# The shared expert of a mixture of experts moved behind the routed experts, in a one-core kernel of two transformer blocks

## The chip, the core and the metric

The kernel runs on one core of a Trainium2 chip. A core has a matmul engine (TensorE; PE in the profile, with its weight loads as PEld), a vector engine (VectorE, DVE), an activation engine (ScalarE, ACT), a general engine (GpSimd, POOL), a queue engine that issues most of the transfers (SyncE, SP), and sixteen DMA engines that all issuing engines share. The metric is the device time of the whole program in microseconds (us), lower is better. All times of the trace count from the start of the span.

## The reference, cut to what matters

Two blocks follow each other on 512 rows of 1024 columns. The first ends in a mixture of experts; the second is a different transformer block (two layers) that starts from the first one's output. The part that the change touches, cut:

```python
x = layernorm(DN_ALPHA * x + g1 * mix, ln1_w, ln1_b)
h = layernorm(x) * (1 + sc2) + sh2
scores = sigmoid(h @ router_w)          # 512 x 64, 8 experts of 64 are chosen for each row
...
def body(acc, blk):                     # blocks of 128 rows of one expert
    tok, wt, e = blk
    xb = h[tok]
    hid = silu(xb @ w1[e]) * (xb @ w3[e])
    return acc.at[tok].add(wt[:, None] * (hid @ w2[e]))
routed = scan(body, zeros(h.shape), blocks)
shared = (silu(h @ sw1) * (h @ sw3)) @ sw2
x = layernorm(DN_ALPHA * x + g2 * (routed + shared), ln2_w, ln2_b)
```

The shared expert has the size of one routed expert (1024 to 256 and back), but works on all 512 rows, four tiles of 128.

## The kernel before

Each 128 x 128 by 512 product is made of three passes over fp32 data that was split in a high and a low part (`mm3`, lines 128 to 130). A weight granule is 1 MB (128 x 2048 fp32): SyncE loads it (L1181), ScalarE casts its high part (L122), VectorE subtracts to get the low part (L123). An expert has three granules: two for gate and up (`hidden`, 24 matmuls of 128 x 512, the `gu` tiles), one for down (`down`, 12 matmuls, the `y` tiles). Raw granules live in a small ring, and a load waits until the split has freed its slot.

`mix_out` is the stage between the token mixer and the experts. Its steps stand in the tuple `MIX`: load and split the output projection's weights (`l`, `w`, four granules `wo0` to `wo3`), transpose its inputs (`y`), load x and row vectors (`m`), project (`o`), normalise a tile (`n`: x, then h, which goes to `hrows` in DRAM), transpose h (`t`), route it (`r`: the `rt` matmuls, the selection of 8 experts on VectorE, the prefix matmuls `pl`, `place`), begin the first expert (`b`: the selection of its 128 rows, `sel`, and the gather), and load (`e`) and split (`E`) the first experts' granules early. The shared expert has steps of its own here: `L` and `W` load and split its granules `shg0` to `shg2`, and `("s", t)` does row tile t from the transposed h that the router also uses, and writes the result `yosh` to `yrows[0]`, and x to `yrows[1]`. A scheduler then sets the order on each engine, so the tuple is not the order of execution.

Then come 65 jobs in 39 groups: four static experts (e0 to e3), ranked ones, and pairs that share one gather. A group gathers 128 rows of h from `hrows` by a GpSimd DMA (L1690, tile `xg`), transposes them (`tsp`, 8 matmuls) and splits them (`xh`, `xl`); each job multiplies; VectorE scales the result by `g2b` (`yo`, L1444); a GpSimd DMA adds the rows into `yrows[b % 2]` (L1694). Behind e1's first matmuls the experts are put in order of their counts (`cnts`, `ot`, `ord`), and SyncE reads from it which weights to load for the ranked experts (`ids`).

After the last pair (e63, e64, with the down granule `eg2`) a loop for overflowing experts is passed (L1636), which runs no iteration here. Then `combine` loads `yrows[1]` into x (L1610) and `yrows[0]` into y (L1613), adds them (L1618), and normalises (`l2st`, `l2rs`); the second block's first steps (`nm0d`, `nm0p`, `pi`) follow.

Of the kernel before, what the change touches and what calls it, by code (L numbers as in the profile page):

```python
# [13 lines left out]
F32 = mybir.dt.float32  # L14
F32R = mybir.dt.float32r
# [4 lines left out]
OP = mybir.AluOpType  # L20
# [4 lines left out]
P = 128  # L25
D = 1024
KT = D // P
# [3 lines left out]
NT = T // P  # L31
# [26 lines left out]

MIX = (
# [6 lines left out]

STEPS = (
# [26 lines left out]
class Kernel:  # L94
# [1097 lines left out]
        return self.parts(self.load(src, name))  # L1192


    def mix_out(self, cx, shared, begin):
        nc, I = self.nc, self.I
        V, G = nc.vector, nc.gpsimd
        hp = self.hp = self.pool("hp", ctx=cx)
        rp = self.pool("rt", ctx=cx)
        r2 = self.pool("rt2", bufs=2, ctx=cx)  # L1200
        w = [None] * NT
        yT = [[hp.tile([P, KT, P], F32R, tag=f"T{i}{t}", name=f"y{i}{t}") for i in range(2)] for t in range(NT)]
        tensors = {}
        self.hT = [None] * NT

        def load(g):
            w[g] = self.load(I["w_out1_pack"][:, g * 2048:(g + 1) * 2048], f"wo{g}")

        def parts(g):
            w[g] = self.parts(w[g])  # L1210

        def loads():
            for t in range(NT):
                nc.sync.dma_start(self.x[:, t], I["x"][0, t * P:(t + 1) * P, :])
            row = lambda n, ap: self.rowvec(rp, n, ap)
            g1b = rp.tile([P, D], F32, tag="gate", name="g1b")
            nc.sync.dma_start(g1b, self.mods[0:1, :].to_broadcast([P, D]))
            rows = [g1b] + [row(n, ap) for n, ap in (("ln1w", I["ln1_w"]), ("ln1b", I["ln1_b"]), ("sh2b", self.mods[1:2, :]),
                                                     ("sc2b", self.mods[2:3, :]), ("rb", I["router_b"]))]
            tensors.update(zip(("g1b", "lw", "lb", "sh2b", "sc2b", "rb"), rows))  # L1220
            rw = r2.tile([P, D], F32, tag="hr", name="rw", bufs=1)[:, :512].rearrange("p (k n) -> p k n", k=KT)
            tensors["rh"], tensors["rl"] = [rp.tile([P, KT, 64], F32R, name=n) for n in ("rwh", "rwl")]
            nc.sync.dma_start(rw, I["router_w"][0].rearrange("(k p) n -> p k n", p=P))
            self.split(tensors["rh"], tensors["rl"], rw)

        def out(t, g):
            gs = slice(g * 256, g * 256 + 256)
            pm = self.acc(f"wo{g}{t}")[:, :256]
            for k in range(KT):
                c = slice(k * 256, k * 256 + 256)  # L1230
                self.mm3(pm, yT[t][0][:, k], yT[t][1][:, k], w[g][0][:, c], w[g][1][:, c], k == 0, k == KT - 1)
            tm = r2.tile([P, 256], F32, tag="mt", name=f"mt{g}{t}")
            V.tensor_tensor(tm, pm, tensors["g1b"][:, gs], OP.mult)
            V.scalar_tensor_tensor(self.x[:, t, gs], self.x[:, t, gs], ALPHA, tm, OP.mult, OP.add)

        hs = [None] * NT

        def norm(t):
            x = self.x[:, t]
            self.normalize(r2, x, x, tensors["lw"], tensors["lb"], "l1")  # L1240
            h = hs[t] = r2.tile([P, D], F32, tag="hr", name=f"h{t}", bufs=1)
            self.normalize(r2, h, x, tensors["sc2b"], tensors["sh2b"], "lh")
            nc.scalar.activation(x, x, AF.Copy, scale=ALPHA)
            nc.sync.dma_start(self.hrows[t * P:(t + 1) * P, :], h)

        def turn(t):
            self.hT[t] = [hp.tile([P, KT, P], F32R, tag=f"T{i}{t}", name=f"h{i}{t}") for i in range(2)]
            self.transpose_split(self.hT[t][0], self.hT[t][1], [hs[t]])

        def gate():  # L1250
            self.g2b = rp.tile([P, D], F32, tag="gate", name="g2b1")
            nc.sync.dma_start(self.g2b, self.mods[3:4, :].to_broadcast([P, D]))
        do = {"l": load, "m": loads, "y": lambda t: self.transpose_split(yT[t][0], yT[t][1], [self.ymix[:, t]]), "w": parts, "o": out,
              "n": norm, "t": turn, "r": lambda t: self.route(t, r2, *(tensors[n] for n in ("rb", "rh", "rl"))), "g": gate,
              "b": begin, **shared}
        for f, *a in MIX:
            do[f](*a)

# [109 lines left out]
    def moe(self):  # L1368
# [5 lines left out]
        E = 64  # L1374
# [18 lines left out]
        with ExitStack() as c2:  # L1393
            self.grans(self.pool("ew", ctx=c2), 2, 5)
            es = self.pool("es", bufs=2, ctx=c2)
            xg = [es.tile([P, D], F32, name="xg0", bufs=1)]
            G.memset(xg[0], 0.0)
            late = []

            def job(name, gr, x, put, wt=None, first=True, last=True):  # L1400

                hid = self.hidden(name, gr, es, *x, wt)
                if late:
                    late.pop()()
                late.append(lambda: sums.append(self.down(name, gr[2], es, hid, put, () if first else sums[-1], first, last)))
# [30 lines left out]
            def putter(name, end):  # L1436

                yo = []

                def put(half, py):  # L1440
                    if half == 0:
                        yo.append(es.tile([P, D], F32, tag="yo", name="yo" + name))
                    hs = slice(half * 512, half * 512 + 512)
                    V.tensor_tensor(yo[0][:, hs], py, self.g2b[:, hs], OP.mult)  # L1444
                    if half == 1:
                        end(yo[0])
                return put

            src = lambda w: [w[:, i * 2048:(i + 1) * 2048] for i in range(3)]
            with ExitStack() as c3:  # L1450
                sh = []

                def shared_load(i):
                    sh.append(self.load(src(I["sh_pack"])[i], f"shg{i}"))

                def shared_parts(i):
                    sh[i] = self.parts(sh[i])

                def shared(t):

                    rows = slice(t * P, (t + 1) * P)
                    nc.sync.dma_start(self.yrows[1][rows, :], self.x[:, t])

                    def end(y):
                        nc.sync.dma_start(self.yrows[0][rows, :], y)
                    job(f"sh{t}", sh, self.hT[t], putter(f"sh{t}", end))
                shared = {"L": shared_load, "W": shared_parts, "s": shared, "e": first_load, "E": first_parts}
                self.mix_out(c3, shared, begin)
            self.grans(self.pool("ew2", ctx=c2), 4, 0, False)
            op = self.pool("os", ctx=cx, side="right")  # L1470
            self.ordered(op)
# [5 lines left out]
            for n, (b, c, h) in enumerate(jobs):  # L1477
# [32 lines left out]
                if not new:  # L1510
                    late.pop()()
            old[0].append(self.gran(old[1], "eg2"))
            late.pop()()
        cp = self.pool("cmb1", ctx=cx, side="right")
        self.ln2 = [self.rowvec(cp, n, I[n]) for n in ("ln2_w", "ln2_b")]
# [87 lines left out]
    def combine(self, loaded, done):  # L1603

        nc = self.nc
        V, G = nc.vector, nc.gpsimd
        with self.mcx as cx:
            m2 = self.pool("cmb", bufs=NT, ctx=cx, side="right")
            for t in range(NT):
                nc.sync.dma_start(self.x[:, t], self.yrows[1][t * P:(t + 1) * P, :])  # L1610
            ys = [m2.tile([P, D], F32, tag="y0", name=f"y0{t}") for t in range(NT)]
            for t in range(NT):
                nc.sync.dma_start(ys[t], self.yrows[0][t * P:(t + 1) * P, :])  # L1613
            loaded()
            lw, lb = self.ln2
            for t in range(NT):
                x = self.x[:, t]
                V.tensor_tensor(x, x, ys[t], OP.add)  # L1618
                if t < 2:
                    self.normalize(m2, x, x, lw, lb, "l2")  # L1620
                else:
                    mu, rs = self.ln_stats(m2, x, LN_EPS, "l2")
                    V.scalar_tensor_tensor(x, x, mu, lw, OP.subtract, OP.mult)
                    nc.scalar.activation(x, x, AF.Copy, scale=rs)
                    G.tensor_tensor(x, x, lb, OP.add)
                done(t)
# [670 lines left out]
```

## Time and profile before

| what | value |
|---|---|
| time, median of 3 runs | 2931.78 us (2930.54 to 2935.34) |
| profiled execution: time, span | 2929.51 us, 2927.7 us |
| busy share of the span: PE, DVE, ACT, POOL | 90%, 64%, 43%, 17% |
| mean granted TensorE clock | 0.954 |
| PE in the chain that ended last | 38% of the span |
| bytes moved by DMA | 431.72 MB |

The shares are means over a span with very different stages: the mixer comes first, the routing stage lies at about 650 to 780 us, the experts at 780 to 1440, the second block from 1450 on. So a stage has to be read by itself. In a timeline a row gives the start, the duration, the engine, the line, the operation with its output and inputs, and in brackets how long the engine stood idle before it and what ended the wait.

### The profile page before, as it was taken

What the parts mean: (1) busy time and instruction counts of PE and PEld (TensorE: products, weight loads), DVE (VectorE), ACT (ScalarE), POOL (GpSimd) and SP (SyncE); (2) the same over time, 40 slices, a digit from 0 to 9 for tenths busy, and PEclk for the clock granted to TensorE, in tenths of its full rate; (3) what the DMA queues carried; (4) which work ended last, traced back from release to release, by engine and by line L of the source; (5) the groups of instructions that cost most, each with busy time, mean ns of one, the idle gap of its engine ahead of it and who ended that gap; (6) DMA issues with size and microseconds to landing.
All of it is one profiled execution on the core that took longest, in us unless ns stands there. A gap on an engine that the chain in (4) does not pass through costs nothing.

```text
span 2927.7 us, 46888 instructions
## 1 busy us (share of the span) xinstructions
PE 2648.7 (90%) x18599; PEld 2253.6 (77%) x18603; DVE 1876.5 (64%) x3467; ACT 1263.8 (43%) x1976; POOL 491.2 (17%) x510
## 2 busy tenths in 40 slices
PE   6999776779899999999679999999998999999998
PEld 4788565668677877777579899887878988987786
DVE  6973768768789999999769744323337964433323
ACT  4233432323356776667455554222225556322221
POOL 1001332121132123222133410000002431000000
PEclk9999786989899999999889999999999999999999
DMA  6541001215589999999721112222232111223222
GB/s 217 189 153 59 3 25 34 37 38 224 214 296 366 389 377 359 346 374 361 249 89 66 58 51 80 87 83 97 75 108 94 59 59 66 73 92 103 86 88 78
DMA packets 135502, 431.72 MB, mean 147 GB/s; under 512 B 51323, under 2 KB 77883, under 8 KB 96881
## 3 DMA queue, kind: packets, MB, share of 16 engines
q1 hardware_dynamic: 124048, 395.96, 37.4%
q0 software_dynamic: 11232, 32.74, 4.5%
q8 instruction: 147, 2.41, 0.3%
q14 instruction: 75, 0.61, 0.1%
HBM read 400.35 MB, written 36.47 MB: 149 GB/s over the span
## 4 chain that ended last, share of the span: by engine, by line
PE 38%; DVE 6%; POOL 3%; ACT 2%; issue 2%; DMA 0%; POOLq 0%; ACTq 0%; SPq 0%; DVEq 0%
PE ffu L128 3%; PE ffu L129 3%; PE ffu L130 3%; PE ffg L130 3%; PE ffg L129 3%; PE ffg L128 3%; PE dn L129 3%; PE dn L130 2%; PE dn L128 2%; PE po L1967 2%; DVE sc L1933 1%; PE wo L129 1%; PE wo L130 1%; PE pT L1963 1%; PE wo L128 1%
## 5 line engine op out<-in xcount | busy, mean ns | idle before, releaser
L1694 POOL DMA_INDIRECT yrows<-yo,idx x39 | 94.8, 2432 | 352.0 <-DVE yo L1444 178.6
L2073 DVE TENSOR_TENSOR hd<-hd,ffu 128x512 f32<-128x512 f32 x44 | 30.3, 689 | 177.6 <-PE ffu L130 177.6
L1690 POOL DMA_INDIRECT xg<-hrows,idx x39 | 73.5, 1886 | 173.2 <-PE tsp L1149 122.8
L122 ACT CAST hh<-hd 128x512 fp32r<-128x512 f32 x44 | 27.2, 618 | 109.5 <-DVE hd L2073 109.5
L137 POOL TENSOR_TENSOR nm1s<-nm1s,cst 128x1 f32<-128x1 f32 x4 | 2.2, 549 | 381.7 <-DVE nm1s L136 373.8
L137 POOL TENSOR_TENSOR frss<-frss,cst 128x1 f32<-128x1 f32 x4 | 2.2, 549 | 371.6 <-DVE frss L136 371.6
L2092 DVE TENSOR_TENSOR x<-x,dn 128x512 f32<-128x512 f32 x32 | 21.9, 686 | 66.0 <-PE dn L130 66.0
L871 PE MATMUL qa<-PR,qk 64*64 64x128 f32 (+1 forms) x384 | 27.9, 376 | 32.0 <-DVE PR L977 12.6
L1965 ACT COPY pTs<-pT 128x128 f32<-128x128 f32 (+3 forms) x96 | 39.8, 427 | 35.6 <-PE pT L1963 33.4
L2072 ACT ACTIVATE hd<-ffg 128x512 f32<-128x512 f32 x44 | 26.0, 591 | 67.2 <-PE ffg L130 67.0
L1149 PE MATMUL tsp<-cst,xg 128*128 128x128 f32 x312 | 46.1, 284 | 9.2 <-DMA xg<-hrows,idx 9.2
L1932 DVE MAX8 m<-sc 128x8 f32<-128x256 f32 (+2 forms) x96 | 52.9, 555 | 1.0
L123 DVE TENSOR_TENSOR xl<-tsp,xh 128x512 fp32r<-128x512 f32 x78 | 50.9, 683 | 2.4 <-ACT xh L122 2.2
L1933 DVE MATCH_REPLACE8 sc<-m,sc 128x256 f32<-128x256 f32 (+2 forms) x96 | 52.1, 543 | 0.0
L237 DVE SCALAR_TENSOR_TENSOR adas<-adar,cs,adas 128x256 f32<-128x256 f32 x112 | 50.0, 476 | 1.3
L1719 PE MATMUL nm0p<-nm0d,x 128*128 128x128 f32 x64 | 15.0, 424 | 39.4 <-DVE l2rs L136 27.6
L122 ACT CAST xh<-tsp 128x512 fp32r<-128x512 f32 x78 | 42.8, 590 | 18.0 <-PE tsp L1149 18.0
L871 PEld LDWEIGHTS qa<-PR,qk 64*64 64x64 f32 x384 | 19.7, 201 | 35.8 <-issue 14.3
L1967 PE MATMUL po<-va,pTs 128*128 128x64 f32 x320 | 45.0, 275 | 1.0 <-ACT pTs L1965 0.3
L1719 PEld LDWEIGHTS nm0p<-nm0d,x 128*128 128x128 f32 x64 | 13.8, 325 | 40.9 <-DVE l2rs L136 28.3
L1967 PEld LDWEIGHTS po<-va,pTs 128*128 128x128 f32 x320 | 40.3, 191 | 6.0 <-ACT pTs L1965 5.2
L1149 PEld LDWEIGHTS tsp<-cst,xg 128*128 128x128 f32 x312 | 35.9, 145 | 11.6 <-issue 9.6
(4409 smaller groups left out, 10441.2 us busy)
## 6 DMA issues: line engine op xcount, KB each, us to landing
adar<-in_ada_w_dram SPq DMA_DIRECT2D x16, 1024.0 KB
x<-in_w_in_pack_dram SPq DMA_DIRECT2D x11, 1024.0 KB
adaw<-in_ada_w_dram SPq DMA_DIRECT2D x8, 1024.0 KB
x<-in_x_dram SPq DMA_DIRECT2D x8, 512.0 KB
xs<-x SPq DMA_DIRECT2D x8, 512.0 KB
x<-xs SPq DMA_DIRECT2D x8, 512.0 KB
yrows<-x SPq DMA_DIRECT2D x4, 512.0 KB
hrows<-h SPq DMA_DIRECT2D x4, 512.0 KB
```

The lines of the kernel that those rows point to most:

```text
L122: nc.scalar.copy(h, src)
L123: nc.vector.tensor_tensor(l, src, h.bitcast(F32), OP.subtract)
L128: mm(out, ah, bh, start=start, stop=False)
L129: mm(out, ah, bl, start=False, stop=False)
L130: mm(out, al, bh, start=False, stop=stop)
L237: V.scalar_tensor_tensor(acc, wt[:, k], c, acc, OP.mult, OP.add)
L1149: nc.tensor.transpose(pt[:, (k - k0) * w + j * P:(k - k0) * w + (j + 1) * P], x[:, k * P:(k + 1) * P], self.ident)
L1690: self.nc.gpsimd.indirect_dma_start(out=x, out_offset=None, in_=self.hrows, in_offset=bass.IndirectOffsetOnAxis(ap=idx, axis=0), bounds_ch ...
L1694: self.nc.gpsimd.indirect_dma_start(out=self.yrows[i], out_offset=bass.IndirectOffsetOnAxis(ap=idx, axis=0), in_=y, in_offset=None, bounds ...
L1932: V.max(m8, s)
L1933: V.match_replace(s, m8, s, PICKED)
L1967: nc.tensor.matmul(out, st[:, s], v[:, s, c0:c0 + w], start=(s == 0), stop=(s == n - 1))
```

## The change

The four shared steps leave `MIX`; e0's and e1's granules are loaded and split in places where the shared ones stood. Behind the last pair, the rows of h are read back from `hrows` tile by tile, transposed and split again, and the shared expert runs as four more jobs, whose result stays in the x tile on the chip. `yrows[1]` now begins as x, written in `norm`; `yrows[0]` begins as zeros, written by four DMAs from the zeroed `xg` tile. `combine` loads both sums for each tile, and adds both.

```diff
 MIX = (
...
-    ("o", 0, 0), ("o", 1, 0), ("o", 2, 0), ("o", 3, 0), ("L", 0), ("W", 0), ("L", 1), ("W", 1), ("L", 2),
+    ("o", 0, 0), ("o", 1, 0), ("o", 2, 0), ("o", 3, 0), ("e", 0, 0), ("E", 0), ("e", 0, 1), ("E", 1), ("e", 1, 0),
...
-    ("t", 0), ("r", 0), ("n", 1), ("o", 3, 1), ("o", 3, 2), ("o", 3, 3), ("t", 1), ("r", 1), ("n", 2), ("g",), ("W", 2), ("s", 0),
-    ("t", 2), ("r", 2), ("n", 3), ("s", 1), ("t", 3), ("r", 3), ("b",), ("e", 0, 0), ("E", 0), ("e", 0, 1), ("E", 1), ("e", 1, 0), ("e", 1, 1),
-    ("s", 2), ("s", 3))
+    ("t", 0), ("r", 0), ("n", 1), ("o", 3, 1), ("o", 3, 2), ("o", 3, 3), ("t", 1), ("r", 1), ("n", 2), ("E", 2), ("e", 1, 1),
+    ("t", 2), ("r", 2), ("n", 3), ("t", 3), ("r", 3), ("b",))
...
             nc.sync.dma_start(self.hrows[t * P:(t + 1) * P, :], h)
+            nc.sync.dma_start(self.yrows[1][t * P:(t + 1) * P, :], x)
...
             G.memset(xg[0], 0.0)
+            for t in range(NT):
+                nc.sync.dma_start(self.yrows[0][t * P:(t + 1) * P, :], xg[0])
...
-                def shared(t):
...
-                    nc.sync.dma_start(self.yrows[1][rows, :], self.x[:, t])
...
-                        nc.sync.dma_start(self.yrows[0][rows, :], y)
-                    job(f"sh{t}", sh, self.hT[t], putter(f"sh{t}", end))
...
             old[0].append(self.gran(old[1], "eg2"))
+
+            def shared_putter(t):
+
+                def put(half, py):
+                    hs = slice(half * 512, half * 512 + 512)
+                    V.tensor_tensor(self.x[:, t, hs], py, self.g2b[:, hs], OP.mult)
+                return put
+            w = src(I["sh_pack"])
+            gr = [self.gran(w[i], f"shg{i}") for i in range(2)]
+            for t in range(NT):
+                x = xg[(len(groups) + t) % 2]
+                nc.sync.dma_start(x, self.hrows[t * P:(t + 1) * P, :])
+                xh = ep.tile([P, KT, P], F32R, tag="xh", name=f"xhs{t}")
+                xl = ep.tile([P, KT, P], F32R, tag="xl", name=f"xls{t}")
+                self.transpose_split(xh, xl, [x])
+                job(f"sh{t}", gr, (xh, xl), shared_putter(t))
+                if t == 0:
+                    gr.append(self.gran(w[2], "shg2"))
             late.pop()()
...
             for t in range(NT):
-                nc.sync.dma_start(self.x[:, t], self.yrows[1][t * P:(t + 1) * P, :])
-            ys = [m2.tile([P, D], F32, tag="y0", name=f"y0{t}") for t in range(NT)]
-            for t in range(NT):
-                nc.sync.dma_start(ys[t], self.yrows[0][t * P:(t + 1) * P, :])
+                for i in range(2):
+                    nc.sync.dma_start(ys[t][i], self.yrows[i][t * P:(t + 1) * P, :])
...
-                V.tensor_tensor(x, x, ys[t], OP.add)
+                V.tensor_tensor(x, x, ys[t][0], OP.add)
+                V.tensor_tensor(x, x, ys[t][1], OP.add)
```

In SyncE's queue the four writes of zeros stand between the loads of the projection's first two granules, `wo0r` and `wo1r`, which were neighbours before. Line numbers are one lower after the change from `MIX` on.

The first place is SyncE's queue from the last row of h (`hrows`) that the routing stage writes. `yrows_7124` is `yrows[0]`. Before:

```order
L1244 DMA hrows<-h_8100 128x1024
L1465 DMA yrows_7124<-yosh_8156 128x1024
L1465 DMA yrows_7124<-yosh_8354 128x1024
L1530 DMA ocst<-in_oconsts_dram 128x321
L1155 DMA g2b<-mods 128x1024
L1181 DMA e1o2r<-in_exp_pack_dram 128x2048
L1181 DMA e2g0r<-in_exp_pack_dram 128x2048
L1465 DMA yrows_7124<-yosh_8408 128x1024
L1181 DMA e2g1r<-in_exp_pack_dram 128x2048
L1181 DMA e2o2r<-in_exp_pack_dram 128x2048
```
After the change, from the same place (`yrows_7125` is `yrows[1]`):

```order
L1244 DMA yrows_7125<-x 128x1024
L1243 DMA hrows<-h_8078 128x1024
L1180 DMA e3g1r<-in_exp_pack_dram 128x2048
L1180 DMA e1o2r<-in_exp_pack_dram 128x2048
L1180 DMA e2g0r<-in_exp_pack_dram 128x2048
L1530 DMA ocst<-in_oconsts_dram 128x321
L1154 DMA g2b<-mods 128x1024
L1180 DMA e2g1r<-in_exp_pack_dram 128x2048
L1180 DMA e2o2r<-in_exp_pack_dram 128x2048
```
The writes of the shared results (`yosh`) are gone from between the loads of e1's to e3's granules, and e3's first two granules have moved ahead of e1's third.

The second place is ScalarE between the last routing step and the sort of the experts (`otr` is the copy that the sort waits for). Before:

```order
L122 CAST sh3th<-sh3ht 128x256
L122 CAST xh_8466<-tsp 128x512 x2
L122 CAST e2g0h<-e2g0r 128x2048
L1340 ACTIVATE e0hid<-e0gu 128x256
L122 CAST e2g1h<-e2g1r 128x2048
L122 CAST e1o2h<-e1o2r 128x2048
L1569 COPY otr_8564<-ot_8563 64x512
L1569 COPY otr_8575<-ot_8574 64x512
```
After the change, from the end of the routing steps on:

```order
L121 CAST e1o2h<-e1o2r 128x2048
L121 CAST xh_8267<-tsp 128x512 x2
L121 CAST e2g0h<-e2g0r 128x2048
L1337 ACT_TABLE_LOAD
L1337 ACTIVATE e0hid<-e0gu 128x256
L1569 COPY otr_8340<-ot_8339 64x512
L121 CAST e2g1h<-e2g1r 128x2048
L1569 COPY otr_8351<-ot_8350 64x512
```
The shared hidden casts and activations are gone, one table load stands ahead of `e0hid`, and the first `otr` copy stands directly behind `e0hid`, ahead of the cast of e2's second granule.

The third place is VectorE at the end of the last pair. Before, the last two scaled results (`yo`) are followed by the loop's register load:

```order
L1344 SCALAR_TENSOR_TENSOR e64hid<-e64hid,wt_14530,e64gu 128x256
L123 TENSOR_TENSOR e63tl<-e63ht,e63th 128x256
L123 TENSOR_TENSOR e64tl<-e64ht,e64th 128x256
L1444 TENSOR_TENSOR yo_15098<-e63y_15065,g2b 128x512
L1444 TENSOR_TENSOR yo_15098<-e63y_15072,g2b 128x512
L1635 TENSOR_LOAD ntot
```
After the change:

```order
L1341 SCALAR_TENSOR_TENSOR e64hid<-e64hid,wt_14302,e64gu 128x256
L122 TENSOR_TENSOR e63tl<-e63ht,e63th 128x256
L122 TENSOR_TENSOR xls_14871<-tsp,xhs_14870 128x512 x2
L122 TENSOR_TENSOR shg2l<-shg2r,shg2h 128x2048
L122 TENSOR_TENSOR e64tl<-e64ht,e64th 128x256
L1339 TENSOR_TENSOR sh0hid<-sh0hid,sh0gu 128x256
L1443 TENSOR_TENSOR yo_14927<-e63y_14837,g2b 128x512
L1443 TENSOR_TENSOR yo_14927<-e63y_14844,g2b 128x512
L122 TENSOR_TENSOR xls_14947<-tsp,xhs_14946 128x512 x2
L122 TENSOR_TENSOR sh0tl<-sh0ht,sh0th 128x256
L1339 TENSOR_TENSOR sh1hid<-sh1hid,sh1gu 128x256
L1500 TENSOR_TENSOR x<-sh0y_14997,g2b 128x512
```
Behind the last pair's hidden product the transposed rows of h are split (`xls`), the shared granules too, and the four shared jobs' products follow (three more of them behind this piece) ahead of the loop's register load.

## Rows read from the trace of the kernel before

**Rows 1.** Windows: length, busy us of five engines, clock granted, DMA share, GB/s.

```profile
720.00:800.00 80.00, 65.13 (x339) 52.64 (x338) 60.27 (x200) 27.58 (x34) 9.10 (x7) 0.83 0.55 201
800.00:860.00 60.00, 54.84 (x292) 43.81 (x291) 50.11 (x92) 34.31 (x34) 18.09 (x9) 0.91 0.83 277
860.00:1400.00 540.00, 514.97 (x2627) 415.62 (x2626) 509.63 (x585) 371.82 (x337) 138.78 (x63) 1.00 1.00 368
1440.00:1460.00 20.00, 0.00 (x0) 0.00 (x0) 7.72 (x11) 1.18 (x1) 3.09 (x2) 0.55 0.84 304
```

**Rows 2.** The same view in two windows of 5 us.

```profile
730.00:735.00 5.00, 5.00 (x21) 4.62 (x21) 5.00 (x17) 3.00 (x5) 3.79 (x1) 0.50 0.26 83
770.00:775.00 5.00, 0.34 (x9) 0.25 (x8) 4.35 (x6) 2.21 (x3) 0.00 (x0) 0.79 1.00 403
```

**Rows 3.** Timeline of VectorE in the routing stage.

```profile
736.91 2.27 DVE L123 TENSOR_TENSOR e0g1l<-e0g1r,e0g1h 128x2048 fp32r<-128x2048 f32 x1
...
749.25 0.41 DVE L1342 TENSOR_TENSOR sh1hid<-sh1hid,sh1gu 128x256 f32<-128x256 f32 x1
...
752.01 0.68 DVE L1444 TENSOR_TENSOR yosh<-sh0y,g2b 128x512 f32<-128x512 f32 x1
...
762.83 0.23 DVE L1297 TENSOR_TENSOR place<-pl,mask 128x64 f32<-128x64 f32 x1 [1.62 <-PE pl L1296]
```

**Rows 4.** Timelines of TensorE and of GpSimd there: start, us, operation, wait.

```profile
727.05 0.40 PE L128 MATMUL rt<-rwh,h 128*128 128x64 f32 x1
...
738.76 0.28 PE L129 MATMUL rt<-rwl,h 128*128 128x64 f32 x1
...
766.67 1.27 POOL L1690 DMA_INDIRECT xg<-hrows,idx  x1 [21.07 <-DVE idx L1329]
...
776.28 1.09 PE L1149 MATMUL tsp<-cst,xg 128*128 128x128 f32 x4 [5.94 <-DMA xg<-hrows,idx]
```

**Rows 5.** Timeline of SyncE's DMA queue, routing stage.

```profile
653.83 0.43 SPq L1181 DMA_DIRECT2D wo1r<-in_w_out_pack_dram  x1
...
767.29 0.38 SPq L1181 DMA_DIRECT2D e2g0r<-in_exp_pack_dram  x1
...
782.51 0.33 SPq L1465 DMA_DIRECT2D yrows<-yosh  x1
...
782.93 0.38 SPq L1181 DMA_DIRECT2D e2g1r<-in_exp_pack_dram  x1
```

**Rows 6.** Timelines of TensorE and ScalarE from the first expert to the sort.

```profile
788.95 0.39 PE L130 MATMUL e0gu<-e0g1h,xl 128*128 128x512 f32 x1
...
791.31 0.43 PE L1559 MATMUL cnts<-perm,cntc 64*128 64x64 f32 x2
...
792.04 1.89 ACT L122 CAST e1o2h<-e1o2r 128x2048 fp32r<-128x2048 f32 x1
...
793.84 0.57 ACT L1569 COPY otr<-ot 64x512 f32<-64x512 f32 x1
...
794.46 1.10 PE L1571 MATMUL ord<-perm,otr 64*128 64x64 f32 x8 [1.94 <-ACT otr L1569]
```

**Rows 7.** Timeline of TensorE in the last two pairs.

```profile
1413.69 1.04 PE L1149 MATMUL tsp<-cst,xg 128*128 128x128 f32 x8
...
1425.96 0.39 PE L128 MATMUL e64gu<-e63g0h,xh 128*128 128x512 f32 x1
...
1431.18 0.39 PE L130 MATMUL e64gu<-e63g1h,xl 128*128 128x512 f32 x1
...
1438.65 0.39 PE L130 MATMUL e63y<-eg2h,e64tl 128*128 128x512 f32 x1
```

**Rows 8.** Chain of waits behind the last expert: start, us, what.

```profile
1440.05 7.87 DMA yrows<-yo,idx
...
1448.85 3.63 DMA y<-yrows
...
1452.51 1.24 DVE x L1618
```

More of the change, by code (lines that the diff above doesn't have):

```diff
@@ L1192, in gran, with mix_out @@
         return self.parts(self.load(src, name))
-    def mix_out(self, cx, shared, begin):
+    def mix_out(self, cx, ahead, begin):
         nc, I = self.nc, self.I
@@ L1248, in turn @@
             self.transpose_split(self.hT[t][0], self.hT[t][1], [hs[t]])
-        def gate():
-            self.g2b = rp.tile([P, D], F32, tag="gate", name="g2b1")
-            nc.sync.dma_start(self.g2b, self.mods[3:4, :].to_broadcast([P, D]))
         do = {"l": load, "m": loads, "y": lambda t: self.transpose_split(yT[t][0], yT[t][1], [self.ymix[:, t]]), "w": parts, "o": out,
-              "n": norm, "t": turn, "r": lambda t: self.route(t, r2, *(tensors[n] for n in ("rb", "rh", "rl"))), "g": gate,
-              "b": begin, **shared}
+              "n": norm, "t": turn, "r": lambda t: self.route(t, r2, *(tensors[n] for n in ("rb", "rh", "rl"))),
+              "b": begin, **ahead}
         for f, *a in MIX:
@@ L1450, in moe @@
             with ExitStack() as c3:
[L1451 to L1457, printed above, removed]
-                def shared(t):
-                    rows = slice(t * P, (t + 1) * P)
-                    nc.sync.dma_start(self.yrows[1][rows, :], self.x[:, t])
-                    def end(y):
-                        nc.sync.dma_start(self.yrows[0][rows, :], y)
-                    job(f"sh{t}", sh, self.hT[t], putter(f"sh{t}", end))
-                shared = {"L": shared_load, "W": shared_parts, "s": shared, "e": first_load, "E": first_parts}
-                self.mix_out(c3, shared, begin)
+                self.mix_out(c3, {"e": first_load, "E": first_parts}, begin)
             self.grans(self.pool("ew2", ctx=c2), 4, 0, False)
@@ L1608, in combine @@
             m2 = self.pool("cmb", bufs=NT, ctx=cx, side="right")
+            ys = [[m2.tile([P, D], F32, tag=f"y{i}", name=f"y{i}{t}") for i in range(2)] for t in range(NT)]
             for t in range(NT):
-                nc.sync.dma_start(self.x[:, t], self.yrows[1][t * P:(t + 1) * P, :])
-            ys = [m2.tile([P, D], F32, tag="y0", name=f"y0{t}") for t in range(NT)]
-            for t in range(NT):
-                nc.sync.dma_start(ys[t], self.yrows[0][t * P:(t + 1) * P, :])
+                for i in range(2):
+                    nc.sync.dma_start(ys[t][i], self.yrows[i][t * P:(t + 1) * P, :])
             loaded()
```

## The prediction

> **What bounds the kernel now.** I read the windows first, because a mean over the span hides the stages. From 860 to 1400 us the experts run with the DMA engines at 1.00 of their time and 368 GB/s, TensorE busy for 514.97 of 540 us and VectorE for 509.63 [rows 1]. Three limits lie so close together there that nothing can be packed in: work that is added behind the experts is paid in full, and a later or earlier start of this stage comes through to its end. The stage before, 720 to 800 us, is different: TensorE is busy for 65.13 of 80 us, VectorE for 60.27, the DMA engines for 0.55 [rows 1]. No engine is full; it is a chain of small steps (route a tile, select, gather, first expert, sort) with the shared expert's matmuls in its gaps. After the experts comes a hole: TensorE does nothing from 1440 to 1460 us [rows 1].
>
> So the question is what the shared expert costs where it stands now (little of its TensorE time, some of the chain) against what it costs behind the experts (all of it), less the part of the hole that it fills. Next I read the timelines of the chain and of the hole, and last SyncE's queue.
>
> **The cost at the end.** One 128x512 matmul follows the other every 0.227 us: the first of e64's 24 starts at 1425.96, the last at 1431.18, 5.22 us for 23 steps [rows 7]. A shared job has 36 of them, 8.17 us, and two transposes of the hidden rows, about 0.2; its rows of h need eight transposes, 1.04 us as in the pair before [rows 7]. Four jobs: 4 x (8.17 + 0.2 + 1.04) = 37.6 us, with a little waiting **+38 us**. What could hide it? The last pair's own waits are short, since TensorE runs at nearly full share up to them. Nothing else follows that doesn't need the result. From below: if all four sets of transposes fall into waits, 34. From above: the shared weights are three more granules for a DMA that is already full (3 MB at 368 GB/s [rows 1], 8.5 us) and three more splits of 2.27 us on VectorE [rows 3], ahead of which e64's hidden product may queue; if all three splits show, 38 + 6.8, so 45. I take 38, since eg2 is the last routed granule, and its load is over well before the last pair's matmuls are.
>
> **The hole.** The last matmul starts at 1438.65 [rows 7]; then the last scatter-add takes 7.87 us until it has landed, the loop is passed, the load of y takes 3.63 us from 1448.85, and the first addition starts at 1452.51 [rows 8]. That is 13.9 us. After the change that scatter-add runs beside the shared jobs (38 us against 7.87, a safe cover). What remains: the end of the last matmul (0.39), a product on VectorE (0.68, as the row of `yosh` [rows 3]), the step from the scatter's end at 1447.92 to the load (0.9), and the load 3.63 [rows 8]: 5.6, say 6.4 with a wait. **-7.5 us**. Bounds: -3 if eight loads instead of four ahead of the additions take some 4 us longer, -10 if the load partly overlaps the loop.
>
> **The additions.** Each tile now has two of 1.24 us [rows 8]. Before the first statistics two more stand on VectorE, some 2.5 us later; but VectorE isn't full here (7.72 of 20 us [rows 1]) and the x loads, half of the traffic, are replaced by loads that can run early. I take 0 (-3 to +3).
>
> **The gain in front.** The experts' start hangs on the row numbers (idx) of the first group; the gather is issued at 766.67 and its rows reach TensorE at 776.28 [rows 4]. On VectorE the shared expert puts ahead of idx one granule's split more (2.27), five instructions like the hidden product (0.41) and four scaled results (0.68) [rows 3]: 2.27 + 2.05 + 2.72 = 7.0 us. VectorE also waited 1.62 us for prefix matmuls (`pl`) that stand among shared ones on TensorE [rows 3]. Two things go against it. The zeros are 2 MB in SyncE's queue between the first two granules of the output projection; at the 403 GB/s of a window with full engines [rows 2] that is 5.2 us of transfer, of which I charge 1.5, as the projection starts on wo0 (0 to 5.2). And TensorE loses the work that fills its gaps: the routing matmuls come every 0.21 us in the window that was granted 0.50 of the clock (the 1.2 GHz level), each taking 0.40, and take 0.28 at full clock [rows 2, 4]. The 24 of a tile take about 2.5 us longer there, 5 for two more tiles, of which a part shows. So idx comes 5 us earlier (2 to 8).
>
> The Trainium skill says in TensorE: Matmul & The Clock Gate, section What's actually happening, that the throttled state is the default and activity releases it, which speaks against taking these matmuls out; this trace agrees, at a granted clock of 0.50 in that window [rows 2].
>
> Then the first expert. From its transposes at 776.28 [rows 4] to its last gate-and-up matmul at 788.95 [rows 6] are 12.7 us; it needs 8 transposes (1.04), a cast, a split and a wait of about 1.8, and 24 x 0.227 = 5.45, so 8.3. The rest, 4.4, are shared products between its own. Behind it the rest of sh3's product stands until `cnts` at 791.31, 2.3 us [rows 6]. The copy `otr` for the sort starts at 793.84 behind the cast of e1's third granule (1.89, from 792.04) and one like it [rows 6]; in the new order it stands directly behind e0's activation, which saves about 1.3. Sum at the sort: 5 + 4.4 + 2.3 + 1.3 = 13.0. SyncE agrees: after 767.29 its queue stands until 782.51 for a shared result, and e2's second granule is behind it [rows 5]; without these waits the loads start up to 15 us earlier. The gather itself isn't shorter: it took 9.6 us [rows 4], now with loads beside it.
>
> The Trainium skill says in DMA: Bandwidth & Descriptors, section Issuing engines are not separate DMA queues, that transfers of all issuing engines interleave on the same sixteen; by it, earlier weight loads slow the first gather, and if it took 3 us more, the gain would be 10.
>
> Since the experts then run at the limits named above, the gain stays: **-13 us** (5 to 22).
>
> **Sum.** 38 - 7.5 + 0 - 13 = +17.5 us. On the profiled execution's 2929.5 us that is 2947.0. Its time lies 2.3 us below the median of the runs shown; on the median it is 2949.3. I say 2949, 0.6% slower.
>
> **The rivals.**
>
> *Faster: the routing stage is bound by TensorE after all.* The shared jobs take 4 x 8.17 = 33 of the 65.13 busy us there, and the DMA engines are idle for 36 of 80 us [rows 1]. If the experts started 33 to 36 us earlier, the sum would be 38 - 7.5 - 35 = -4.5, 2927 on the median; it is faster from a start 30.5 us earlier on. For it: TensorE is the busiest engine there, and the wait for `pl`. Against it: the chain of selection on VectorE and the 9.6 us of the gather [rows 3, 4] don't shrink with it. Chance 0.11.
>
> *The front gives little.* TensorE is slow for all four tiles (5 us), the zeros hold up wo1 by their 5.2 us, and the gather comes later beside the loads: 13 falls to 4.5, the sum is +26, 2957. For it: the window at 0.50 [rows 2]. Against it: the waits behind idx are gone whatever the clock does. Chance 0.20.
>
> *The shared weights are late at the end*, by the DMA that is full or the three splits: 38 becomes 45, the sum +24.5, 2956. Chance 0.10.
>
> *Earlier loads give more.* The DMA engines run at 0.83 from 800 to 860 us [rows 1], 10 us of idle time; if they are full from the first expert on, the gain is 22, the sum +8.5, 2940. Chance 0.16.
>
> **How the numbers follow.** My forecast, +12 to +21, has 0.43. A difference of 0.2%, 5.9 us, is about what a measurement of this kernel can tell from none. Of the first rival 0.08 is faster by more and 0.03 within; of the last, 0.06 within or just over. With the bounds of the combine stage: faster 0.09, same 0.10, slower 0.81. The range reaches from 2932 to 2960: it takes in the late weights, the small gain in front and most of the larger one, and leaves out the faster case and mishaps that add up. The likeliest case alone is 2944 to 2953.
>
> **What would show it.** The first gather at about 762 us and the first `cnts` at about 779; e1's later granules without a 15 us stand in SyncE's queue; the same pace as before in the steady stage; the last routed pair's matmuls about 13 us earlier; then some 38 us of shared matmuls at full clock; and 6 to 7 us from the last matmul to the first addition. The prediction is wrong if the first expert starts over 25 us earlier, if the steady stage changes its pace, or if the shared weights make TensorE wait at the end.

## The result and the profile after

The changed kernel takes 2956.91 us in the median of four runs (2952.63 to 2964.51), the one before 2931.16 (2924.83 to 2935.34): 1.0094 times as long, with an interval of 1.007 to 1.0117. The span of the profiled execution is 2950.5 us, 22.8 more than before. The forecast was 2949 with a range of 2932 to 2960; its likeliest case alone, 2944 to 2953, was exceeded.

Windows of the changed kernel, with the columns of [rows 1] and [rows 2]:

```profile
720.00:800.00 80.00, 48.78 (x258) 42.04 (x259) 55.83 (x223) 18.32 (x24) 8.91 (x8) 0.59 0.47 174
...
860.00:1400.00 540.00, 515.66 (x2620) 416.69 (x2619) 509.24 (x576) 373.53 (x336) 137.66 (x62) 1.00 1.00 368
...
1440.00:1460.00 20.00, 19.93 (x95) 15.91 (x94) 6.85 (x12) 3.47 (x8) 0.00 (x0) 1.00 0.20 59
```

The steady stage has nearly the same busy times and the same 368 GB/s as before [rows 1]. The hole at 1440 is filled with matmuls at full clock. New is the first row: TensorE has 16 us less work in the routing stage, and its mean granted clock fell from 0.83 [rows 1] to 0.59.

Timelines of SyncE, VectorE, GpSimd and TensorE of the changed kernel, at the places of [rows 3] to [rows 7]:

```profile
651.42 0.36 SPq L1180 DMA_DIRECT2D wo0r<-in_w_out_pack_dram  x1
653.12 3.30 SPq L1396 DMA_DIRECT2D yrows<-xg  x4
656.46 1.24 SPq L1180 DMA_DIRECT2D wo1r<-in_w_out_pack_dram  x1
...
763.42 0.16 DVE L1326 CAST idx<-sel 128x1 uint32<-128x1 f32 x1
...
763.61 0.38 SPq L1180 DMA_DIRECT2D e2g1r<-in_exp_pack_dram  x1
...
763.88 1.27 POOL L1690 DMA_INDIRECT xg<-hrows,idx  x1 [17.13 <-DVE idx L1326]
...
773.17 1.97 PE L1148 MATMUL tsp<-cst,xg 128*128 128x128 f32 x8 [8.34 <-DMA xg<-hrows,idx]
...
784.54 1.17 PE L1571 MATMUL ord<-perm,otr 64*128 64x64 f32 x8 [0.67 <-ACT otr L1569]
...
1421.13 0.39 PE L129 MATMUL e64gu<-e63g1h,xl 128*128 128x512 f32 x1
...
1466.38 0.39 PE L129 MATMUL sh3y<-shg2h,sh3tl 128*128 128x512 f32 x1
...
1515.55 0.41 PE L127 MATMUL pi<-wi0x0h,nm0h 128*128 128x296 f32 x1 [2.32 <-DVE nm0l L1724]
```

Read alone, these rows mislead: the sort comes 9.9 us earlier than in [rows 6], but already `wo0r`, the last entry of SyncE's queue ahead of the first one that differs, is issued 2.0 us earlier than in the profile of before (653.4), though no engine's order differs ahead of it. In the ten profiles of this study it lies between 648.8 and 657.1 us. So I count from that issue. Timelines of a second profile of the unchanged kernel before:

```profile
654.47 0.36 SPq L1181 DMA_DIRECT2D wo0r<-in_w_out_pack_dram  x1
...
764.82 0.16 DVE L1329 CAST idx<-sel 128x1 uint32<-128x1 f32 x1 [0.35 <-PE sel L1328]
...
1429.01 0.39 PE L130 MATMUL e64gu<-e63g1h,xl 128*128 128x512 f32 x1
...
1491.52 0.39 PE L128 MATMUL pi<-wi0x0h,nm0h 128*128 128x296 f32 x1
```

From 654.47 to `idx` are 110.4 us here, against 112.8 in the first profile of before (766.2 less 653.4): inside the stage, too, two profiles of one kernel differ by up to 3 us. The distances from `wo0r`'s issue in all profiles, each the difference of two starts as above:

| kernel | idx | sort (`ord`) | last routed gate-up | last expert matmul | first addition | first `pi` |
|---|---|---|---|---|---|---|
| before | 112.8 | 141.0 | 777.8 | 785.2 | 799.1 | 839.8 |
| before, again | 110.4 | 138.6 | 774.5 | 782.0 | 796.0 | 837.0 |
| changed | 112.0 | 133.1 | 769.7 | 815.0 | 820.4 | 864.1 |
| changed, again | 111.7 | 132.9 | 768.2 | 813.4 | 818.8 | 862.9 |
| no shared expert | 111.8 | 132.8 | 768.6 | 776.1 | 788.2 | 829.9 |
| zeros early | 106.9 | 128.0 | 766.8 | 812.0 | 817.1 | 861.1 |
| early sum | 112.0 | 133.1 | 770.6 | 815.9 | 821.1 | 862.1 |
| bare matmuls | 108.4 | 129.4 | 764.3 | 809.5 | 814.6 | 858.8 |
| all three | 102.8 | 123.5 | 762.6 | 807.8 | 812.6 | 853.4 |
| one tile at the end | 110.7 | 134.5 | 769.9 | 786.1 | 794.3 | 835.4 |

The ledger, from the means of the two profiles of each kernel: the routed experts end 7.2 us earlier (776.2 to 769.0); from there to the last expert matmul it takes 37.8 us longer (7.5 to 45.3); from that matmul to the first addition 8.5 less (13.9 to 5.4); from there to the second block's first matmul 3.0 more (40.9 to 43.9). The sum is +25.1, which is the difference of the medians, 25.8, within its error. The term of the front is the least certain: by which two profiles are compared, it lies between 4.8 and 9.6. The others repeat within 0.5.

### The profile page after: what moved, and what is told of

Read it like the earlier page. It is cut to its first block, busy times and chain, and to the rows that moved or that the text cites. A ratio compares the mean times of both kernels' runs of the same rounds, so it can differ in the third digit from the quotient of the medians.

```text
span 2950.5 us, 46989 instructions
## 1 busy us (share of the span) xinstructions
PE 2654.9 (90%) x18635; PEld 2262.1 (77%) x18635; DVE 1889.9 (64%) x3479; ACT 1264.7 (43%) x1980; POOL 493.9 (17%) x510
## 4 chain that ended last, share of the span: by engine, by line
PE 37%; DVE 6%; POOL 3%; ACT 2%; issue 2%; DMA 0%; POOLq 0%; ACTq 0%; DVEq 0%; SPq 0%
PE ffu L127 3%; PE ffu L129 3%; PE ffu L128 3%; PE ffg L129 3%; PE ffg L128 3%; PE ffg L127 3%; PE dn L128 2%; PE dn L129 2%; PE dn L127 2%; PE po L1967 2%; PE wo L128 1%; PE wo L129 1%; PE pT L1963 1%; PE wo L127 1%; DVE sc L1933 1%
## 5 line engine op out<-in xcount | busy, mean ns | idle before, releaser
L122 DVE TENSOR_TENSOR hl<-hd,hh 128x512 fp32r<-128x512 f32 x44 | 30.3, 688 | 13.7 <-ACT hh L121 13.7
```

The lines of the kernel that those rows point to most:

```text
L122: nc.vector.tensor_tensor(l, src, h.bitcast(F32), OP.subtract)
```

## The experiments

All are compared with runs of the kernel before on the same chip; the ratios have 95% intervals.

**No shared expert.** The four jobs, their weights and their rows are left out, so the shared part of the result is missing.

```diff
-            def shared_putter(t):
...
-            gr = [self.gran(w[i], f"shg{i}") for i in range(2)]
-            for t in range(NT):
...
-                job(f"sh{t}", gr, (xh, xl), shared_putter(t))
```

> The changed kernel without the shared expert's four jobs at the end, their weights and their rows of h (the shared part of the result is left out). The changed trace has its last routed gate-and-up matmul 10.0 us earlier than before, its last matmul 27.7 us later and the first addition 19.3 us later. Theory A (the sum holds: the shared jobs cost 37.8 us of TensorE at the end and fill 8.4 us of the hole, and the front gained 8 to 10 us by their leaving): the time falls by 29 us, to about 2928 on the median, 3 us under the kernel before. Rival B (the front gained nothing; the 10 us are a difference between two runs, since 2.0 of them lie ahead of the output projection already): the last matmul lies at the place of before, 1436 to 1439, and the time is that of before or up to 3 us over it, 2931 to 2934. Rival C (the shared jobs at the end also slow what follows): below 2922.

Timelines of SyncE and TensorE of this kernel:

```profile
657.11 0.36 SPq L1180 DMA_DIRECT2D wo0r<-in_w_out_pack_dram  x1
...
1425.75 0.39 PE L129 MATMUL e64gu<-e63g1h,xl 128*128 128x512 f32 x1
...
1433.22 0.39 PE L129 MATMUL e63y<-eg2h,e64tl 128*128 128x512 f32 x1
```

The ratio was 0.9989 (0.9978 to 1.0001): about 3 us under before, as A says, and at the upper edge of its interval also level with it. The trace is clearer than the time. The last expert matmul stands at 776.1 from `wo0r`, 7.5 behind the last routed gate-and-up as before, and 7.5 us earlier than the mean of before. So by the trace the front's gain is there: taking the shared expert out, with the zeros and the cold routing stage left in, gives 7.5 us. To the first `pi` it is 8.5 us ahead of before by the trace, more than the at most 6.4 us that the ratio allows; the rest of this profile, the second block, took 1438.5 us against 1434.5 and 1434.6 in the two profiles of before. Whether that is scatter isn't settled here, so by time alone the front's gain could be smaller.

**Zeros early.**

```diff
             G.memset(zero, 0.0)
...
+            for t in range(NT):
+                nc.sync.dma_start(self.yrows[0][t * P:(t + 1) * P, :].rearrange("p (c n) -> p c n", c=4),
+                                  zero[:, :256].unsqueeze(1).to_broadcast([P, 4, 256]))
...
             G.memset(xg[0], 0.0)
-            for t in range(NT):
-                nc.sync.dma_start(self.yrows[0][t * P:(t + 1) * P, :], xg[0])
```

> The changed kernel with the 2 MB of zeros written some 230 us earlier, inside the token mixer, from a zeroed tile that is there already, so that the second granule of the output projection is loaded right behind the first, as before. Theory A (the zeros are what ate the front's gain: counted from the load of the first projection granule, the first row tile of h is written 4.4 us later after the change than before): the h rows and the first gather come 3 to 4 us earlier, and so does the end: 2953 on the median. Rival B (VectorE and the cold TensorE set the time from the second tile on, and the zeros' delay is made up by the fourth tile): first h row 4 us earlier, first gather within 1 us, time within 1 us of the changed kernel, 2956 to 2957.

Timelines of SyncE and VectorE of this kernel:

```profile
652.99 0.36 SPq L1184 DMA_DIRECT2D wo0r<-in_w_out_pack_dram  x1
653.39 0.43 SPq L1184 DMA_DIRECT2D wo1r<-in_w_out_pack_dram  x1
...
759.90 0.16 DVE L1330 CAST idx<-sel 128x1 uint32<-128x1 f32 x1
```

`wo1r` follows at once again, and the row numbers come 4.9 us sooner after `wo0r` than in the changed kernel (106.9 against 111.9): A, and not B, in the routing stage. The edit changes VectorE's order too, but what VectorE waited for between `wo0r`'s issue and `idx` points the same way. Waits (total us, times, longest) of the changed kernel:

```profile
DVE wo1l L122 <- ACT wo1h L121: 4.8, 1, 4.8
DVE wo3l L122 <- ACT wo3h L121: 4.5, 1, 4.5
DVE wo2l L122 <- ACT wo2h L121: 0.2, 1, 0.2
```

and of this one:

```profile
DVE wo2l L122 <- ACT wo2h L121: 3.5, 1, 3.5
DVE wo3l L122 <- ACT wo3h L121: 1.4, 1, 1.4
```

The waits for the projection's granules fell from 9.5 to 4.9 us. Of the 4.9 us at `idx`, 2.2 are left at the last routed gate-and-up (766.8 against 769.0) and 2.4 at `pi`. The ratio, 1.008 (1.0061 to 1.01), can't be told from the changed kernel's.

**Early sum.**

```diff
                     V.tensor_tensor(self.x[:, t, hs], py, self.g2b[:, hs], OP.mult)
+                    V.tensor_tensor(self.x[:, t, hs], self.x[:, t, hs], yb[t][:, hs], OP.add)
...
+                yb[t] = es.tile([P, D], F32, tag="yo", name=f"yb{t}")
+                nc.sync.dma_start(yb[t], self.yrows[1][t * P:(t + 1) * P, :])
...
-                V.tensor_tensor(x, x, ys[t][0], OP.add)
-                V.tensor_tensor(x, x, ys[t][1], OP.add)
+                V.tensor_tensor(x, x, ys[t], OP.add)
```

> The changed kernel with the rows of the sum that begins as x loaded tile by tile while the shared jobs run, and added there in halves behind each shared product, so that the last stage loads four tiles and adds four, as before. Theory A (the doubled additions and loads of the last stage are the 3.0 us that the second block starts later after the first addition than before): from the first addition to the first pi matmul 40.7 us instead of 43.7, and 3 to 4 us less in all, 2953 on the median. Rival B (the additions lie beside other waits of the last stage, and the 3.0 us come from the order of its tiles): no more than 1 us. Rival C (the additions in halves delay the shared products on VectorE, and TensorE waits for accumulators): slower by 1 to 3 us.

From the first addition of the last stage to the first `pi` it took 41.0 us, as before, instead of 43.7 and 44.0: the 3.0 us hang on the doubled additions and their loads (A). The shared jobs took no longer for the extra halves (45.3 us from the last routed gate-and-up to the last matmul, as without). VectorE of the changed kernel shows why two additions stand on the path:

```profile
1471.84 1.23 DVE L1617 TENSOR_TENSOR x<-x,y 128x1024 f32<-128x1024 f32 x1 [2.60 <-DMA y<-yrows]
1473.10 1.23 DVE L1618 TENSOR_TENSOR x<-x,y 128x1024 f32<-128x1024 f32 x1
1474.24 1.22 DVE L1617 TENSOR_TENSOR x<-x,y 128x1024 f32<-128x1024 f32 x1
1475.37 1.28 DVE L144 BATCH_NORM_STATS2 l2st<-x 128x6 f32<-128x512 f32 x2
```

VectorE of the kernel before, at the same place:

```profile
1452.51 1.23 DVE L1618 TENSOR_TENSOR x<-x,y 128x1024 f32<-128x1024 f32 x1 [2.57 <-DMA y<-yrows]
1453.77 1.29 DVE L145 BATCH_NORM_STATS2 l2st<-x 128x6 f32<-128x512 f32 x2
```

The first statistics start 3.5 us behind the start of the first addition, against 1.3 before: the second addition of tile 0 and the first of tile 1 stand between. But the additions' own length doesn't explain the 3.0 us. The kernel without the shared expert has the same doubled additions, and its statistics start as late (3.5 us); yet from the first addition to `pi` it took 41.6 us, only 0.7 over before. What the doubled additions cost depends on what follows them, and how isn't shown. The ratio is 1.0089 (1.0069 to 1.0109); its routing stage, with the zeros in place, was as slow as the changed kernel's.

**Bare matmuls.** Their sums are read by nobody.

```diff
+        def bare(t):
+            pg = self.acc(f"bare{t}")
+            for k in range(KT):
+                c = slice(k % 4 * 512, k % 4 * 512 + 512)
+                self.mm3(pg, self.hT[t][0][:, k], self.hT[t][1][:, k], ahead["g"][k // 4][0][:, c], ahead["g"][k // 4][1][:, c], k == 0, k == KT - 1)
...
-    ... ("n", 2), ("E", 2), ("e", 1, 1),
-    ("t", 2), ("r", 2), ("n", 3), ("t", 3), ("r", 3), ("b",))
+    ... ("n", 2), ("E", 2), ("j", 0), ("e", 1, 1),
+    ("t", 2), ("r", 2), ("n", 3), ("j", 1), ("t", 3), ("r", 3), ("b",), ("j", 2))
```

> The changed kernel with 72 bare matmuls of 128x512 in the routing stage, 24 on each of the first three tiles of h with the first expert's weights, whose sums nobody reads: TensorE has about the shared expert's gate-and-up work there again, without its activations, hidden products, second products and stores. Theory A (the routing stage lost time by TensorE's half clock: routing passes of 0.21 us instead of 0.11): the granted clock returns to 0.9 or more in 720 to 760 us, the first gather comes 2 to 4 us earlier, and the time falls by as much, to 2953. Rival B (the half clock isn't on the path, and the matmuls of the shared expert were themselves in the way): the first gather 0 to 4 us later, and the time 0 to 5 us longer, 2957 to 2962.

Windows of the changed kernel:

```profile
720.00:740.00 20.00, 12.74 (x59) 12.03 (x59) 18.35 (x62) 3.63 (x6) 1.10 (x2) 0.60 0.32 118
740.00:760.00 20.00, 10.73 (x63) 9.87 (x63) 14.60 (x78) 2.74 (x6) 1.45 (x2) 0.50 0.51 197
```

and of the one with the bare matmuls:

```profile
720.00:740.00 20.00, 17.55 (x97) 15.31 (x96) 18.21 (x54) 3.75 (x7) 2.01 (x2) 0.83 0.32 111
740.00:760.00 20.00, 14.30 (x100) 11.28 (x98) 17.95 (x110) 4.26 (x5) 3.71 (x3) 0.81 0.64 227
```

The granted clock rose from 0.60 and 0.50 to 0.83 and 0.81, not quite to the 0.9 that A names, and the row numbers came 3.4 us sooner (108.4 against 111.9), the last routed gate-and-up 4.7, although TensorE had 72 matmuls more to do. The edit also changes VectorE's order here, so the path from the clock to `idx` has to be followed. The routing matmuls of the last three tiles come every 0.21 us in the changed kernel; here those of the last two come every 0.11. VectorE's waits for the router's scores between `wo0r`'s issue and `idx`, in the changed kernel:

```profile
DVE sel L1267 <- ACT s L1266: 6.5, 3, 2.7
```

and with the bare matmuls:

```profile
DVE sel L1273 <- ACT s L1272: 1.8, 2, 1.3
```

With early zeros alone this wait is 6.5 us, as in the changed kernel. So the half clock is on the path. The ratio, 1.009 (1.007 to 1.0111), doesn't show it; behind `pi` this profile took 1439.4 us, against 1435.0 to 1436.6 in the five others with all shared jobs at the end.

**Before and changed, again.** Both unchanged.

> The kernel before, unchanged, for a second profile of it. The first projection granule was issued at 653.4 us in its first profile and at 649.6 to 657.1 in the five others, though nothing that they execute ahead of it differs but four zero writes in one. Theory: this is scatter between runs; here too it lies somewhere in 649 to 658, while the distances inside the stages repeat: from that issue to the first gather's row numbers 112.8 us, to the last routed gate-and-up matmul 777.8, from the last expert matmul to the first pi matmul 54.5, each within 1 us. Rival: the distances scatter by 3 us or more as well, and the differences between the kernels' front stages can't be read from one profile each.

> The changed kernel, unchanged, on the same chip as the others of this set. The time is 1.0070 to 1.0117 times that of before, as in its own comparison. Distances as in its first profile, within 1 us each: from the first projection granule's issue to the row numbers 112.0 us, to the last routed gate-and-up matmul 769.7, 37.8 us of shared jobs behind the last routed matmul's place, from the last shared matmul to the first pi matmul 49.1. Rival: the front gain of 8 us is scatter, and this profile shows 775 or more to the last routed gate-and-up matmul.

Before measured 1.0 (0.9988 to 1.0011) against itself. Its distance to `idx` was 2.4 us less than in the first profile and the one to the last routed gate-and-up 3.3 less, so the rival holds in part: a single profile of before tells the front only to 3 us. From the last expert matmul to `pi` it repeats within 0.5. The changed kernel repeats within 1.6 us everywhere, at 1.0088 (1.0073 to 1.0103).

**All three.** Zeros early, early sum and bare matmuls together, the three edits shown.

> The changed kernel with the zeros written in the mixer, the first sum added within the shared jobs, and the 72 bare matmuls in the routing stage. Alone they took 3.0, 2.9 and 4.8 us from the distance between the first projection granule's issue and the first pi matmul. Theory A (the three terms are apart from each other): 10 to 11 us less than the changed kernel, that distance 853 to 854 us, 1.004 to 1.006 times the time of before: the move stays slower, since 37.8 us at the end are more than the hole and the whole of the front. Rival B (zeros and clock are one cost, as the stage has one path): 6 to 8 us less, 1.0065.

Timelines of SyncE, VectorE and TensorE of this kernel:

```profile
652.05 0.36 SPq L1184 DMA_DIRECT2D wo0r<-in_w_out_pack_dram  x1
...
754.88 0.16 DVE L1336 CAST idx<-sel 128x1 uint32<-128x1 f32 x1
...
1505.46 0.59 PE L127 MATMUL pi<-wi0x0h,nm0h 128*128 128x296 f32 x1
```

1.0041 (1.0026 to 1.0055): the three together are apart from the changed kernel also in time, by 0.0047, some 14 us. The distance to `pi` is 853.4, 10.1 less than the changed kernel's 863.5, against 10.7 expected; `idx` comes 9 us sooner (102.8), and 8.7 sooner than before. So A: zeros and clock are two costs. And with both of them and the additions taken away, the moved shared expert is still some 12 us slower by the ratio (15 by the distance) than the one in front.

VectorE adds it up. Windows from `wo0r`'s issue to `idx`, with the columns of [rows 1], of before, changed, early zeros, bare matmuls and all three:

```profile
653.42:766.20 112.78, 103.57 (x678) 93.74 (x679) 91.91 (x255) 39.63 (x43) 12.92 (x10) 0.88 0.52 193
651.42:763.42 112.00, 82.97 (x569) 79.70 (x569) 86.12 (x245) 31.74 (x33) 10.86 (x11) 0.76 0.56 213
652.99:759.90 106.91, 83.14 (x569) 80.22 (x569) 86.18 (x245) 31.75 (x33) 10.65 (x11) 0.76 0.54 204
649.59:758.04 108.45, 93.21 (x641) 86.84 (x641) 86.47 (x245) 31.68 (x33) 12.76 (x11) 0.88 0.59 220
652.05:754.89 102.84, 89.19 (x641) 82.92 (x641) 86.30 (x246) 31.42 (x33) 12.54 (x11) 0.91 0.56 212
```

VectorE (the third pair) is the busiest engine of this stretch in the changed kernel. The move took 5.8 us of work from it (91.91 to 86.12), and its idle time grew by 5.0, from 20.9 to 25.9. The three repairs leave its work at 86 us and take only idle time: 20.7 with early zeros, 22.0 with the bare matmuls, 16.5 with all.

**One tile at the end.** The kernel before, with the last row tile alone moved.

```diff
-    ("s", 2), ("s", 3))
+    ("s", 2))
...
             old[0].append(self.gran(old[1], "eg2"))
...
+            x = xg[len(groups) % 2]
+            nc.sync.dma_start(x, self.hrows[t * P:, :])
...
+            gr = [self.gran(w[i], f"shz{i}") for i in range(2)]
+            job("sh3", gr, (xh, xl), put)
+            gr.append(self.gran(w[2], "shz2"))
             late.pop()()
```

> The kernel before with only the last of the four row tiles of the shared expert moved behind the last pair, its rows read back, the three weight granules loaded a second time, and its quarter of the sum set to zero in the mixer; the other three tiles stay in front. Theory A (the hole of 13.9 us behind the last matmul is filled by one job at next to no cost, and the front gives part of its gain): 9.6 us more of matmuls, 8.4 less of hole, 1 more of additions, 2 to 4 less in front: 0 to 2 us faster than before, a ratio of 0.9993 to 1. Rival B (the weights that are loaded again for one job, or the hidden rows that wait for their splits, make TensorE wait at the end): 3 us or more slower. Rival C (the front gives nothing, since the sort waits for something else than sh3): 2 to 3 us slower.

0.9999 (0.9986 to 1.0011): level with before. By the distances the sort comes 5.3 us sooner than the mean of before, the last expert matmul 2.5 later, and `pi` 3.0 sooner; the measurement can't tell that from nothing. B's 3 us lie at the very edge of the interval, and C's 2 to 3 inside it; by the trace both are out. The hole isn't filled to its end:

```profile
1434.87 0.39 PE L130 MATMUL sh3y<-shz2h,sh3tl 128*128 128x512 f32 x1
...
1443.12 1.23 DVE L1638 TENSOR_TENSOR x<-x,y 128x1024 f32<-128x1024 f32 x1 [7.12 <-DMA y<-yrows]
```

Between the last matmul and the first addition 8.2 us are left, not 5.4: one job isn't long enough to cover the last scatter-add.

## Why the prediction was right, and where its terms were off

The move is slower for the reason given: behind the experts nothing hides the shared expert, and in front most of it was hidden. The time lies in the upper part of the range, +25.1 by the ledger against +17.5, and beyond the likeliest case (+12 to +21): the two ends were sized well, the front was not.

- *The cost at the end*, +38: measured 37.8. The spacing of 0.227 us and the transposes of [rows 7] were enough to price it. The shared weights weren't late; that rival is out. SyncE issued `shg0` to `shg2` from 1403 to 1410 us, well ahead of the shared matmuls, and the only wait that the profile shows for TensorE among these is 0.5 us, for a cast of the last tile's hidden rows.
- *The hole*, -7.5: measured -8.5. The last scatter-add, 7.87 us in [rows 8], did run beside the shared jobs. What is left isn't the summed chain, though: the load that the first addition waits for is issued at 1467.10, 0.7 us behind the start of the last matmul, and takes 4.72 us, not 3.63; the last product on VectorE (1468.55) isn't in this chain. That the sum comes so close is in part luck.
- *The additions*, "I take 0 (-3 to +3)": measured +3.0, at the edge. The prediction named the 2.5 us on VectorE and set them against earlier loads. The early sum took the 3.0 away again, and in the changed kernel the statistics of the first tile wait behind three additions instead of one. That the additions by themselves cost this much isn't shown, since without the shared expert they cost 0.7.
- *The front*, -13: measured -7.2. Its step "So idx comes 5 us earlier (2 to 8)" is the one that failed: from `wo0r` to `idx` it is 111.9 us after and 111.6 before. What VectorE was freed of is real, 5.8 of the 7.0 us summed. With zeros and clock repaired, `idx` comes 8.7 us sooner than before, against the 7.0 of work and 1.6 of waiting in the prediction. But the zeros, "of which I charge 1.5", took 4.9: the load of `wo1` is on the path. That is nearly the 5.2 of their transfer, but `wo1r` is also issued only 5.0 us behind `wo0r` instead of 0.4 [rows 5]; which of the two sets the delay isn't separated. And the half clock, of whose 5 us "a part shows", took 3.4. Behind `idx` the prediction was nearly right: from the first gather's transposes to the sort 11.4 us instead of 18.2 and 17.8, so -6.6 where 8.0 was summed.

Among the rivals, "the front gives little" named the right two mechanisms, with all of the clock's and the zeros' cost, and took too much: 4.5 of gain, where 7.2 were measured. Its third, a gather that comes later beside the loads, did not happen: from its issue to the first transposes the first gather took 9.3 us in both profiles of the changed kernel, 9.6 and 10.0 before. Its sum, +26, is nearly the measured one by luck, as the 3.0 of the additions, which it leaves out, make up for that. The faster rival is out: with all shared work gone the experts end 7.5 us sooner, and with zeros and clock repaired 13.6 (762.6 against 776.2), not 33, so TensorE's load wasn't the bound of the routing stage. "Earlier loads give more" is out too: SyncE issued e2's second granule at 763.61 us instead of 782.93 [rows 5], 17 us sooner when counted from `wo0r`, but the experts followed the sort, by 7.

What stays open is why the 4.9 us that the early zeros gave at `idx` lose half on the way to the last routed expert, while the bare matmuls' 3.4 grew to 4.7. The traces show where: e2's first matmul still comes 4.7 us sooner (149.8 from `wo0r` against 154.5, the mean of the changed kernel), e5's only 2.6 (186.0 against 188.6), and the kernel with all three edits loses the same 2.3 there. The growth with the bare matmuls is no more than the changed kernel's own two profiles differ by (1.5).

Open, too, is what the doubled additions meet. In the changed kernel one instruction of VectorE behind them, `nm0d` at 1503.88, takes 2.35 us, just while GpSimd works on `x` (1503.82 to 1506.15); without the shared expert, and with the early sum, every `nm0d` ahead of `pi` takes 0.28 or 0.29. Whether that is the rest of the 3.0 us was not tested.

## What to carry to other kernels

Work that sits in the gaps of a latency-bound stage can be cheap there, though it may look like half of that stage's busy time (33 of 65 us in the prediction's count): taking 37.8 us of work out gained 7.2, and 13.6 with zeros and clock repaired. Before such work is moved behind a stage with no slack, price it in full there and take back only the hole that it can cover. An initialisation that seems to be one more store is priced by what is queued behind it: ask which load is next in that queue and who waits for it. And count from a fixed event near the change, not from the start of the span, when the stages ahead scatter by more than the effect.

## What the runs showed of the hardware

Matmuls whose result nobody reads made a chain of small matmuls faster: 72 of 128x512 brought the granted clock in 720 to 760 us from 0.60 and 0.50 up to 0.83 and 0.81, the spacing of the last two tiles' routing matmuls from 0.21 to 0.11 us, and the end of the chain 3.4 us forward. The Trainium skill says in TensorE: Matmul & The Clock Gate, section What's actually happening, that activity releases a throttle that is on by default; these windows agree.

`wo0r`, late in the token mixer, was issued anywhere within 8.3 us (648.8 to 657.1) in ten profiles. In seven of them no engine's order differs up to there; the other three add one or four writes of zeros.
